# Turning the softmax weights of all eight heads of the second attention on VectorE, in a hybrid decoder trunk

## The chip, the core and the metric

The kernel runs on one core of a Trainium2 chip. The core has a matrix engine (TensorE, PE in the profile; PEld is its weight load), three engines for elementwise work (VectorE or DVE, ScalarE or ACT, GpSimd or POOL) and SyncE (SP), which here only issues transfers. Transfers are issued by SyncE and by ScalarE, each from its own list of instructions. Data lies in SBUF (128 partitions); TensorE writes into PSUM, of which this kernel uses eight banks. The metric is the time of one execution on the device, in microseconds.

## The reference

Two layers, each a mixer of three branches and an MLP, over 256 tokens of 1024 numbers:

```
h = rms_norm(x, attn_norm[l])
p = h @ w_in          # cq ckv k_rope | mq mk mv | rq rk rv rg | three gates
merged = sigmoid(g_mla)  * (mla(...)       @ w_branch_mla)
       + sigmoid(g_moba) * (moba(mq,mk,mv) @ w_branch_moba)
       + sigmoid(g_ret)  * (retention(rq,rk,rv,rg) @ w_branch_ret)
x = x + merged @ w_out
x = x + square(relu(rms_norm(x) @ w_mlp_up)) @ w_mlp_down
```

The second attention is `moba`: eight heads of 64. Its block is 256 tokens, as long as the sequence, so what is left of it is causal softmax attention of 256 queries on 256 keys. Retention has four heads with a decay in place of the softmax: scores times decay, times values, then a group norm per head, times silu of `rg`.

## The kernel before, in words

All activations are held turned: 128 rows of the model's dimension in the partitions, 256 tokens along the free axis. A product in full precision is made of three TensorE passes on rounded parts: each weight block comes from memory as `raw`, ScalarE rounds it to `whi` (line 210), VectorE makes the rest `wlo` (line 212), and TensorE adds three matmuls (lines 231 to 233), or, where the output is turned, a wide and a narrow one (lines 412 and 414). There are 7 `raw` buffers and 6 of `whi` and `wlo`. Line 195 is the load of a weight block, issued by SyncE.

The work of a layer is written as a list of units, `prog`, of one weight block each. Attention work is hung behind units with `at(slot, step)`. Around the change the units are, in order: the gates of the second attention (`gmoba1`, 4 blocks), the first attention's output (`bmla0`, `bmla1`, 2 each), retention's queries and keys (`rqk`, 4), its values (`rv`, 4), its gate (`rg`, 4), the second attention's output (`bmoba`, 4) and then retention's mixer gate (`gret`).

What the kernel lists is not the final order. Each engine has one list, fixed when the kernel is built: a planner simulates the engines' times and puts each instruction where its operands are ready by its own estimate, preferring what is written earlier. `keep_in_program_order` pins an instruction behind the one written before it on its engine; `manual_schedule` and, with it, `in_a_row` keep TensorE's part of some steps in the written order.

The second attention does its heads in two groups of four, `first` being the slot of `gmoba1`'s second block. Scores of heads 0 to 3 at `first`, of heads 4 to 7 eight units later (`GAP`). For each head VectorE adds the mask and takes the maximum (lines 498 and 501), ScalarE makes the exponential with its sum (line 507), VectorE divides (line 512): `prob`, 128 queries x 384 (one block for the first 128 queries, two for the others).

The product with the values needs the weights turned, keys in the partitions. There are two ways in the kernel before:

- heads 0 to 3 (`turned_blocks`, `moved_blocks`): VectorE turns 32x32 blocks within each quarter of the partitions (line 523) into one tile `blocks`; then sixteen transfers (line 563) of 32 partitions x 384 numbers, 48 KB each, exchange the blocks between quarters and give `probT`. Eight are issued by SyncE and eight by ScalarE, by turns, all pinned.
- heads 4 to 7 (`turned`): TensorE turns each 128x128 block against the identity, three per head (line 518), into a PSUM bank `ps_pt`, and ScalarE copies it to `probT` (line 519).

The first attention (`group is None`) turns all its heads the second way. `values` (lines 577 and 579) are the products with the values, into a bank `po`.

At the slot of `rg`'s second block one row of TensorE work is written: retention's scores (`ret_scores`, line 481, then line 998 on VectorE multiplies by the decay into `retA`), and then the two `values` steps of the second attention. `ret_values` (lines 1006 to 1008) use `retA` at the slot of `rg`'s last block. Retention's queries and keys pass through a rotation: four transfers each exchange quarters (line 434, `qkoth`), GpSimd and VectorE multiply by the tables and add (lines 446 and 449).

`blocks` lies in the buffer `KK`, of which there is one. It holds in turn the first attention's keys, `blocks`, then `gn` (retention's norm weights, loaded at line 1068 by a pinned SyncE transfer at `rv`'s first slot and used by GpSimd after `rg`), then half of the merged output.

Of the kernel before, what the change touches and what calls it, by code (L numbers as in the profile page):

```python
# [137 lines left out]
def trunk(ctx: ExitStack, tc: tile.TileContext, gx, wts, consts, gfin, gn, xtok, out):  # L138


    nc = tc.nc
# [76 lines left out]
    def acc_tile(name="acc"):  # L218
        return ps.tile([P, 512], F32, name=name, tag="acc", bufs=4)
# [31 lines left out]
    def split_plain(src, hi, lo):  # L251
        return nc.scalar.activation(hi, src, AF.Copy), nc.vector.tensor_sub(lo, src, hi.bitcast(F32))
# [98 lines left out]
    def project(l, key, xn, n, done=None, before=None, turns=(range(NT),)):  # L351

        accs, ws = [], []
        per = where[l, key, 0][1]
        count = KD // per

        def unit(i, ts, j):
            if not accs:
                accs.extend(acc_tile() for _ in range(NT))
            if before:  # L360
                before(i)
            if len(ws) <= j:
                ws.append(load_w(l, key, j))
            wh, wl = ws[j]
            for kk in range(per):
                k = per * j + kk
                ah, al = xn.k(k)
                for t in ts:
                    sl = slice(P * t, P * t + P)
                    three(accs[t][:, :n], ah[:, sl], al[:, sl], wh[:, kk, :], wl[:, kk, :], k == 0, k == KD - 1)  # L370
            if i == count * len(turns) - 1:
                done(accs)

        for turn, ts in enumerate(turns):
            for j in range(count):
                i = turn * count + j
                prog.append(((key, i), lambda i=i, ts=ts, j=j: unit(i, ts, j)))
# [87 lines left out]
    def in_a_row(*jobs):  # L465


        with tc.manual_schedule(engines={mybir.EngineType.PE}):
            rest = [job() for job in jobs]
        for job in rest:  # L470
            job()
# [14 lines left out]
    def attention_head(score, scale):  # L486


        got = {}

        def scores(s_ps=None):
            if s_ps is None:
                s_ps = misc_tile("ps_s")
                score(s_ps[:, 0:P], slice(0, P), slice(0, P))
                score(s_ps[:, P : 3 * P], slice(P, S), slice(0, S))
            p = sb.tile([P, 3 * P], F32, name="prob", bufs=4)
            m = small("smx")
            nc.vector.tensor_tensor_reduce(
                p[:, 0:P], s_ps[:, 0:P], mask[:, P : 2 * P], 1.0, NEG_INF, ALU.add, ALU.max, m[:, 0:1]
            )  # L500
            nc.vector.tensor_tensor_reduce(
                p[:, P : 3 * P], s_ps[:, P : 3 * P], mask, 1.0, NEG_INF, ALU.add, ALU.max, m[:, 1:2]
            )
            nc.vector.tensor_scalar(m[:, 2:4], m[:, 0:2], -scale, None, op0=ALU.mult)  # L504
            spans = ((0, P), (P, 3 * P))
            for i, (a, b) in enumerate(spans):
                nc.scalar.activation(  # L507
                    p[:, a:b], p[:, a:b], AF.Exp, bias=m[:, 2 + i : 3 + i], scale=scale, accum_out=m[:, 4 + i : 5 + i]
                )
            nc.vector.reciprocal(m[:, 6:8], m[:, 4:6])  # L510
            for i, (a, b) in enumerate(spans):
                nc.vector.tensor_scalar(p[:, a:b], p[:, a:b], m[:, 6 + i : 7 + i], None, op0=ALU.mult)
            got["p"] = p

        def turn(dst):
            pt = misc_tile("ps_pt")
            for i, src in enumerate((0, P, 2 * P)):
                nc.tensor.transpose(pt[:, P * i : P * i + P], got["p"][:, src : src + P], ident)  # L518
            nc.scalar.activation(dst, pt[:, : 3 * P], AF.Copy)

        def turn_blocks(dst):

            return nc.vector.transpose(dst, got["p"])

        return scores, turn, turn_blocks

    def attention(oT, score, vs, scale, first, group=None, former=None):

        tiles, pT = {}, {}

        def four_tile(h):
            if h // 4 not in tiles:
                tiles[h // 4] = sb.tile([P, 4 * 3 * P], F32, name="probT", bufs=2)
            return tiles[h // 4]

        def turned(h, turn):
            o = four_tile(h)[:, 3 * P * (h % 4) : 3 * P * (h % 4) + 3 * P]  # L540
            turn(o)
            pT[h] = o[:, 0:S], o[:, S : 3 * P]

        def turned_blocks(h, turn):

            if h == 0:
                pT["blocks"] = sb.tile([P, 4 * 3 * P], F32, name="blocks", tag="KK", bufs=1)
            by_head = (
                z.rearrange("p (c t h j) -> p h t c j", c=4, t=3, h=4)[:, h] for z in (pT["blocks"], four_tile(h))
            )  # L550

            tc.keep_in_program_order(turn(next(by_head)))
            o = next(by_head)
            pT[h] = o[:, 0:2], o[:, 2]

        def moved_blocks():

            e = 3 * P
            for a in range(4):
                for b in range(4):  # L560
                    src = pT["blocks"][32 * a : 32 * a + 32, e * b : e * b + e]
                    queue = (nc.sync, nc.scalar)[b % 2]
                    dma = queue.dma_start(four_tile(0)[32 * b : 32 * b + 32, e * a : e * a + e], src)
                    tc.keep_in_program_order(dma)

        def values(h0):


            o, v = acc_tile("po"), vs()
            for h in (h0 + 2, h0):  # L570
                cs = slice(S * (h - h0) // 2, S * (h - h0) // 2 + S)
                for i in range(2):
                    for j in (1, 0):
                        vh = v[i][:, VD * (h + j) : VD * (h + j) + VD]
                        dst = o[64 * j : 64 * j + 64, cs]
                        if i == 0:
                            nc.tensor.matmul(dst, vh, pT[h + j][0], start=True, stop=False)  # L577
                        else:
                            nc.tensor.matmul(dst[:, P:S], vh, pT[h + j][1], start=False, stop=True)
            dst = (part[:, h0 // 2 : h0 // 2 + 2, :].rearrange("p k s -> p (k s)") for part in oT)  # L580
            return lambda: split_plain(o, *dst)


        blocks = [lambda: values(4), lambda: values(0)]
        heads = [attention_head(lambda o, qs, ks, h=h: score(h, o, qs, ks), scale) for h in range(8)]
        if group is None:
            for h, (scores, turn, _) in enumerate(heads):
                at(first + h, scores)
                at(first + h + 2, lambda h=h, turn=turn: turned(h, turn))
            return blocks  # L590

        def four(h0):
            banks = group(h0)

            def rest():
                for h, bank in enumerate(banks, h0):
                    heads[h][0](bank)

            return rest


        at(first, lambda: in_a_row(*former, lambda: four(0)))
        at(first + GAP, lambda: in_a_row(lambda: four(4)))
        for h in range(4):
            at(first + TURN + h // 2, lambda h=h: turned_blocks(h, heads[h][2]))
            at(first + GAP + 3 + h // 2, lambda h=h + 4: turned(h, heads[h][1]))
        at(first + TURN + 1, moved_blocks)
        return blocks[::-1]

    def gates(l, key, xn):  # L610
# [52 lines left out]
    c = slice(G_END - 2 * KD, G_END + S)  # L663
# [35 lines left out]
    def at(slot, step):  # L699
        steps.setdefault(slot, []).append(step)  # L700

    def slot(key, j):
        return [k for k, _ in prog].index((key, j))
# [9 lines left out]
    def layer(l, xn, before):  # L713

        c0 = []
        c, mla, mqkv, rqkv = {}, {}, {}, {}
# [216 lines left out]
        first = slot("mv", 3)  # L933
# [23 lines left out]
        first = slot("gmoba1", 1)  # L957
        at(first, lambda: omobaT.extend((t4("omobah"), t4("omobal"))))

        def moba_scores(h0):  # L960
# [6 lines left out]
            return banks  # L967

        moba_last = attention(omobaT, None, lambda: mqkv["mv"], MB_D**-0.5, first, moba_scores, mla_last)


# [14 lines left out]
        rT, or_ps, aT, rg, oret = [], [], {}, {}, []  # L986
# [81 lines left out]
            tc.keep_in_program_order(nc.sync.dma_start(rg["gn"], src))  # L1068

        project(l, "rg", xn, 512, rg_done)  # L1070
        at(slot("rv", 0), load_gn)
        branch(l, "bmoba", omobaT, th_moba, merged)
        th_ret = gates(l, "gret", xn)
        order_out = ExitStack()
# [17 lines left out]
                merged_turn(0, i - 1)  # L1092

        branch(l, "bret", oretT, th_ret, merged, between)
        at(slot("rg", 1), lambda: in_a_row(ret_scores, *moba_last))
        for h in range(RT_H):
            at(slot("rg", 3), lambda h=h: ret_values(h))
        at(slot("rg", 3), group_norm)
# [218 lines left out]
    for l in range(L):  # L1317
        xn, before = layer(l, xn, before)
# [6 lines left out]
AHEAD = 1  # L1325
GAP = 8

TURN = 6
T4 = 8
RAW = 7  # L1330

# [79 lines left out]
```

## Time and profile before

| | us |
|---|---|
| median of 3 runs | 829.19 (828.47 to 829.30) |
| the profiled execution | 829.56 |
| its span, first to last instruction | 827.8 |
| TensorE busy | 821.3 |
| VectorE busy | 592.6 |
| ScalarE busy | 480.2 |
| GpSimd busy | 97.7 |

The granted TensorE clock is 0.999 of full speed over the span. The span is 1.8 us shorter than the execution, which has a start and an end around it. Rows of a timeline give the start, the time, the engine, the line, the operation, what it writes and reads, and how many instructions were merged into the row; a bracket gives the idle time ahead of it and what ended it. A q behind an engine's name means its list of issues, such as transfers.

### The profile page before, as it was taken

The page shows a single profiled execution, that of the slowest core. Times are in us where ns is not written, and L with a number is a line of the kernel's source. Part 1 is how long each engine was busy: PE and PEld are TensorE (multiplying, and loading weights), DVE is VectorE, ACT ScalarE, POOL GpSimd, SP SyncE. Part 2 cuts the span into 40 slices and gives each one's busy share as a digit, 9 for nine tenths or more (in the row PEclk, how much of TensorE's full clock was granted, in tenths as well). Part 3 has the DMA queues.
Part 4 walks back from the last instruction along what each step waited for, and adds up shares of the span by engine and source line. Part 5 has one row for each costly group of instructions (what it writes and reads, how often), then busy time and mean ns, then how long its engine had stood idle before and what let it go on. Part 6 is the DMA issues. An engine that isn't in the chain of part 4 may idle for free.

```text
span 827.8 us, 12148 instructions
## 1 busy us (share of the span) xinstructions
PE 821.3 (99%) x4339; PEld 699.1 (84%) x4339; DVE 592.6 (72%) x1067; ACT 480.2 (58%) x853; POOL 97.7 (12%) x75
## 2 busy tenths in 40 slices
PE   9999999999999999999999999999999999999997
PEld 7888878888888888888898888888888888888886
DVE  6877887795787566656697976877868766556663
ACT  7677664545556555555686575563555555555552
POOL 0100440230030000000035210023100300000000
PEclk9999999999999999999999999999999999999999
DMA  9966546736456666665557557565565666666611
GB/s 345 342 220 185 186 168 226 241 126 211 146 182 227 187 194 190 192 191 172 178 186 217 190 171 228 158 194 197 167 193 164 213 182 188 191 202 187 194 54 51
DMA packets 48060, 158.07 MB, mean 191 GB/s; under 512 B 6400, under 2 KB 8832, under 8 KB 47744
## 3 DMA queue, kind: packets, MB, share of 16 engines
q1 hardware_dynamic: 46656, 155.84, 59.3%
q10 hardware_dynamic: 1344, 1.46, 0.6%
q8 instruction: 34, 0.56, 0.3%
q14 instruction: 26, 0.21, 0.1%
HBM read 150.98 MB, written 1.05 MB: 184 GB/s over the span
## 4 chain that ended last, share of the span: by engine, by line
PE 99%; DVE 0%; ACT 0%; issue 0%; DVEq 0%
PE acc L231 18%; PE acc L233 18%; PE acc L232 18%; PE pup L1166 14%; PE pup L1168 7%; PE acc L1116 5%; PE acc L412 4%; PE acc L414 2%; PE ps_s L937 1%; PE acc L782 1%; PE ps_pt L518 1%; PE po L577 1%; PE ps_s L481 1%; PE warm L693 0%; PE acc L784 0%; PE pmt L1082 0%
## 5 line engine op out<-in xcount | busy, mean ns | idle before, releaser
L212 DVE TENSOR_TENSOR wlo<-raw,whi 128x1024 fp32r<-128x1024 f32 (+4 forms) x287 | 344.1, 1208 | 167.2 <-ACT whi L210 108.2
L210 ACT ACTIVATE whi<-raw 128x1024 fp32r<-128x1024 f32 (+4 forms) x287 | 290.9, 1023 | 177.4 <-PE acc L233 95.0
L1166 PE MATMUL pup<-xs,whi 128*128 128x512 f32 x504 | 123.5, 390 | 0.0
L233 PE MATMUL acc<-whi,xs 128*128 128x512 f32 (+1 forms) x304 | 119.5, 393 | 0.0
L232 PE MATMUL acc<-wlo,xs 128*128 128x512 f32 (+1 forms) x304 | 118.9, 391 | 0.0
L231 PE MATMUL acc<-whi,xs 128*128 128x512 f32 (+1 forms) x304 | 118.6, 394 | 0.0
L1166 PEld LDWEIGHTS pup<-xs,whi 128*128 128x128 f32 x504 | 93.4, 188 | 18.6
L231 PE MATMUL acc<-whi,sq 128*128 128x512 f32 x256 | 100.1, 391 | 0.0
L232 PE MATMUL acc<-wlo,sq 128*128 128x512 f32 x256 | 99.9, 390 | 0.0
L233 PE MATMUL acc<-whi,sq 128*128 128x512 f32 x256 | 98.5, 389 | 0.0
L1168 PE MATMUL pup<-xs,wlo 128*128 128x256 f32 x504 | 69.6, 283 | 0.0
L1168 PEld LDWEIGHTS pup<-xs,wlo 128*128 128x128 f32 x504 | 66.6, 191 | 3.1
L233 PEld LDWEIGHTS acc<-whi,xs 128*128 128x128 f32 x304 | 57.1, 188 | 11.5 <-issue 0.3
L231 PEld LDWEIGHTS acc<-whi,xs 128*128 128x128 f32 x304 | 57.1, 188 | 11.3 <-issue 0.7
L232 PEld LDWEIGHTS acc<-wlo,xs 128*128 128x128 f32 x304 | 57.1, 188 | 10.9
L233 PEld LDWEIGHTS acc<-whi,sq 128*128 128x128 f32 x256 | 48.0, 188 | 10.1
L1177 ACT ACTIVATE relu<-relu 128x256 f32<-128x256 f32 x64 | 25.5, 409 | 52.9 <-DVE relu L1176 52.9
L231 PEld LDWEIGHTS acc<-whi,sq 128*128 128x128 f32 x256 | 48.2, 188 | 9.2
L232 PEld LDWEIGHTS acc<-wlo,sq 128*128 128x128 f32 x256 | 48.2, 188 | 8.9
L288 POOL TENSOR_TENSOR sqsum<-sqsum,xsq 128x256 f32<-128x256 f32 x16 | 16.8, 1047 | 293.4 <-ACT xs L247 169.8
L507 ACT ACTIVATE prob<-prob,smx 128x128 f32<-128x128 f32 x64 | 28.4, 445 | 34.6 <-DVE smx L504 18.6
L446 POOL TENSOR_TENSOR qkoth<-qkoth,tab 128x512 f32<-128x512 f32 x12 | 23.3, 1944 | 161.1 <-DMA qkoth<-qkraw 161.1
(227 smaller groups left out, 1159.1 us busy)
## 6 DMA issues: line engine op xcount, KB each, us to landing
raw<-wts SPq DMA_DIRECT2D x264, 512.0 KB, 4.2
qkoth<-qkraw SPq DMA_DIRECT2D x48, 64.0 KB, 3.2
raw<-wts SPq DMA_DIRECT2D x5, 464.0 KB, 6.3
dec<-consts SPq DMA_DIRECT2D x2, 1024.0 KB, 7.4
raw<-wts SPq DMA_DIRECT2D x4, 416.0 KB, 3.2
raw<-wts SPq DMA_DIRECT2D x4, 256.0 KB, 4.3
xrow<-xtok SPq DMA_DIRECT2D x4, 256.0 KB, 7.1
gn<-gn SPq DMA_DIRECT2D x2, 512.0 KB, 4.1
```

Source lines behind the costliest of these rows:

```text
L210: nc.scalar.activation(hi[:, cs], raw[:, cs], AF.Copy)
L212: nc.vector.tensor_sub(lo[:, cs], raw[:, cs], hi[:, cs].bitcast(F32))
L231: nc.tensor.matmul(o, ah, bh, start=start, stop=False)
L232: nc.tensor.matmul(o, ah, bl, start=False, stop=False)
L233: nc.tensor.matmul(o, al, bh, start=False, stop=stop)
L412: nc.tensor.matmul(acc, wh[:, k, :], xn.both(k), start=k == 0, stop=False)
L446: mul = on.tensor_mul(*operands)
L507: nc.scalar.activation(p[:, a:b], p[:, a:b], AF.Exp, bias=m[:, 2 + i : 3 + i], scale=scale, accum_out=m[:, 4 + i : 5 + i])
L1116: nc.tensor.matmul(o, a, b, start=half == 0 and i == 0, stop=4 * half + n == KD and i == len(jobs) - 1)
L1166: nc.tensor.matmul(u, w, xm.both(k), start=k == 0, stop=False)
L1168: nc.tensor.matmul(u[:, 0:S], w, xm.k(k)[0], start=False, stop=k == KD - 1)
L1177: nc.scalar.activation(s, s, AF.Square)
```

## The change

Heads 4 to 7 of the second attention are turned like heads 0 to 3. `turned_blocks` now serves all eight, with a fresh tile `blocks` for each group; VectorE's instructions are pinned for the first group alone. `moved_blocks` is called once per group: the first group's sixteen transfers are all issued by SyncE, the second group's by SyncE and ScalarE by turns. The second group is turned at the slots where TensorE turned it before (11 and 12 units after `first`), and moved at the later of them, the slot of `rv`'s second block. `gn` follows in the same buffer, so its load is written at `rg`'s first slot instead of `rv`'s. In the row of TensorE work at `rg`'s second block, the second attention's values come first and retention's scores after them.

```diff
         def turned_blocks(h, turn):
 
-            if h == 0:
+            if h % 4 == 0:
                 pT["blocks"] = sb.tile([P, 4 * 3 * P], F32, name="blocks", tag="KK", bufs=1)
-            by_head = (
-                z.rearrange("p (c t h j) -> p h t c j", c=4, t=3, h=4)[:, h] for z in (pT["blocks"], four_tile(h))
+            turning, o = (
+                z.rearrange("p (c t h j) -> p h t c j", c=4, t=3, h=4)[:, h % 4] for z in (pT["blocks"], four_tile(h))
             )
-
-            tc.keep_in_program_order(turn(next(by_head)))
-            o = next(by_head)
+            turning = turn(turning)
+            if h < 4:
+
+                tc.keep_in_program_order(turning)
             pT[h] = o[:, 0:2], o[:, 2]
 
-        def moved_blocks():
+        def moved_blocks(h0):
...
-                    queue = (nc.sync, nc.scalar)[b % 2]
-                    dma = queue.dma_start(four_tile(0)[32 * b : 32 * b + 32, e * a : e * a + e], src)
+                    queue = nc.scalar if h0 and b % 2 else nc.sync
+                    dma = queue.dma_start(four_tile(h0)[32 * b : 32 * b + 32, e * a : e * a + e], src)
                     tc.keep_in_program_order(dma)
...
-        for h in range(4):
-            at(first + TURN + h // 2, lambda h=h: turned_blocks(h, heads[h][2]))
-            at(first + GAP + 3 + h // 2, lambda h=h + 4: turned(h, heads[h][1]))
-        at(first + TURN + 1, moved_blocks)
+        for i in range(2):
+            for h in range(4):
+                at(first + TURN[i] + h // 2, lambda h=4 * i + h: turned_blocks(h, heads[h][2]))
+            at(first + TURN[i] + 1, lambda i=i: moved_blocks(4 * i))
         return blocks[::-1]
...
-        at(slot("rv", 0), load_gn)
+        at(slot("rg", 0), load_gn)
...
-        at(slot("rg", 1), lambda: in_a_row(ret_scores, *moba_last))
+        at(slot("rg", 1), lambda: in_a_row(*moba_last, ret_scores))
...
-TURN = 6
+TURN = [6, GAP + 3]
```

## Prediction

> **What bounds the kernel now.** I read the page first: busy time by engine, then the chain that ended last, then which engine waits for whom.
>
> ```profile
> span 827.8 us, 12148 instructions
> ...
> PE 821.3 (99%) x4339; PEld 699.1 (84%) x4339; DVE 592.6 (72%) x1067; ACT 480.2 (58%) x853; POOL 97.7 (12%) x75
> ...
> PE 99%; DVE 0%; ACT 0%; issue 0%; DVEq 0%
> ```
>
> TensorE (PE) works for 821.3 of 827.8 us and is 99% of the chain that ended last. So a microsecond of TensorE work taken out is a microsecond of span, as long as nothing TensorE waits for becomes later than its place in TensorE's list. The rest of this text is about those two things: how much TensorE work goes, and whether the new, longer road of the softmax weights still arrives in time. All times below are from layer 0; layer 1 has the same pattern about 408 us later.
>
> The timeline of TensorE, where the transposes of heads 4 to 7 (line 518) stand among the matmuls of retention's value projection, and the same place in layer 1:
>
> ```profile
> 144.88 0.39 PE L231 MATMUL acc<-whi,xs 128*128 128x512 f32 x1
> 145.11 0.40 PE L232 MATMUL acc<-wlo,xs 128*128 128x512 f32 x1
> 145.34 0.49 PE L518 MATMUL ps_pt<-K,prob 128*128 128x128 f32 x3
> 145.59 0.48 PE L233 MATMUL acc<-whi,xs 128*128 128x512 f32 x1
> ...
> 147.28 0.48 PE L233 MATMUL acc<-whi,xs 128*128 128x512 f32 x1
> 147.59 0.40 PE L231 MATMUL acc<-whi,xs 128*128 128x512 f32 x1
> ...
> 552.74 0.40 PE L232 MATMUL acc<-wlo,xs 128*128 128x512 f32 x1
> ...
> 555.45 0.39 PE L232 MATMUL acc<-wlo,xs 128*128 128x512 f32 x1
> ```
>
> The reader is to see starts, not durations: each matmul lasts about 0.39 us, but the next starts 0.23 us after it (144.88 to 145.11).
>
> The timeline of SyncE's and ScalarE's queues and of VectorE over the same stretch, and the durations and landing times of the moves (line 563):
>
> ```profile
> 130.21 6.92 SPq L563 DMA_DIRECT2D probT<-blocks  x8
> 137.24 2.43 SPq L434 DMA_DIRECT2D qkoth<-qkraw  x4
> 140.34 0.46 SPq L195 DMA_DIRECT2D raw<-wts  x1
> 143.60 2.41 SPq L434 DMA_DIRECT2D qkoth<-qkraw  x4
> 146.12 21.29 SPq L195 DMA_DIRECT2D raw<-wts  x10
> ...
> 130.18 7.29 ACTq L563 DMA_DIRECT2D probT<-blocks  x8
> 137.51 0.40 ACT L507 ACTIVATE prob<-prob,smx 128x128 f32<-128x128 f32 x1 [8.24 <-DMA probT<-blocks]
> 141.56 4.86 ACT L210 ACTIVATE whi<-raw 128x1024 fp32r<-128x1024 f32 x5
> 146.31 1.73 ACT L519 ACTIVATE probT<-ps_pt 128x384 f32<-128x384 f32 x4
> ...
> 129.13 1.02 DVE L523 STREAM_TRANSPOSE blocks<-prob 128x384 f32<-128x384 f32 x2
> 134.34 0.37 DVE L504 TENSOR_SCALAR smx<-smx 128x2 f32<-128x2 f32 x4
> 138.53 0.17 DVE L510 RECIPROCAL smx<-smx 128x2 f32<-128x2 f32 x1 [3.83 <-ACT prob L507]
> 141.37 1.50 DVE L512 TENSOR_SCALAR prob<-prob,smx 128x128 f32<-128x128 f32 x2
> 144.65 5.75 DVE L212 TENSOR_TENSOR wlo<-raw,whi 128x1024 fp32r<-128x1024 f32 x5
> 151.59 0.69 DVE L449 TENSOR_TENSOR qkT<-qkT,qkoth 128x512 f32<-128x512 f32 x1 [1.19 <-POOL qkoth L446]
> ...
> SPq L563 <- DMA probT<-blocks: 2.0, 1, 2.0
> ...
> L563 SPq DMA_DIRECT2D probT<-blocks x8: 507/589/657, 130.2 to 136.5; - x8
> ...
> DMA to landing us min/median/max: 1.9/2.1/4.5
> ```
>
> The eight moves that ScalarE issues hold it for 7.3 us (130.18 to 137.47). Head 4's exponential stands behind them, and VectorE stands 3.83 us behind that. TensorE notices none of it.
>
> **The change part by part.**
>
> *Transposes off TensorE.* From 145.11 to 147.59 there are five steps between main matmuls; without the transposes they take 5 x 0.227 = 1.13 us, with them 2.48. So twelve transposes, with the changes to and fro, cost 1.35 us. In layer 1, 552.74 to 555.45 is six steps: 2.71 - 6 x 0.227 = 1.35 again. Both layers: **2.70 us off TensorE.** The reader may be tempted to price 24 transposes by their duration:
>
> ```profile
> L518 PE MATMUL ps_pt<-K,prob x72: 270/272/275, 73.9 to 555.1; 128*128 128x128 f32 x72
> ```
>
> That would be 24 x 0.272 = 6.5 us. I don't take it, since three of them in a row end 0.49 us after the first begins: they overlap. The Trainium skill's page "TensorE: Matmul & The Clock Gate" (Part 4: PE-mode transpose) gives about 275 ns for such a transpose inside a kernel, there for bf16; the trace agrees on the duration, and by it the saving would be an estimated 6.6 us, which the starts here contradict.
>
> *PSUM copies off ScalarE.* Four copies, 1.73 us a layer, go. ScalarE isn't on the chain, so this is worth nothing in the sum.
>
> *Four more block transposes on VectorE.* 4 x 0.51 = 2.0 us a layer by the row at 129.13. What hides it is the idle 3.83 us at 138.53: ScalarE no longer issues moves there, so its exponentials can begin when the maxima are ready (134.34 + 0.37 = 134.7) and not at 137.51, which brings everything after them forward by 2.8 us. If that cover were gone, the five `wlo` splits at 144.65 would start 2.0 us later. The first of them serves the first block of retention's gate. Its place on TensorE follows from the value projection, which begins here:
>
> ```profile
> 136.01 0.40 PE L231 MATMUL acc<-whi,xs 128*128 128x512 f32 x1
> 157.02 1.58 PE L481 MATMUL ps_r<-qkT 64*128 64x256 f32 x16
> 158.53 0.65 PE L577 MATMUL po<-probT,mv 128*64 128x256 f32 x4
> ...
> 161.28 0.50 PE L233 MATMUL acc<-whi,xs 128*128 128x512 f32 x1
> ...
> 163.70 0.38 PE L1006 MATMUL por<-rv,retA 128*128 128x128 f32 x2
> 166.30 0.48 PE L231 MATMUL acc<-whi,omobah 128*128 128x512 f32 x1
> ...
> 158.91 1.94 DVE L998 TENSOR_TENSOR retA<-ps_r,dec 128x384 f32<-128x384 f32 x4
> ```
>
> Four blocks of 12 matmuls are 48 x 0.227 = 10.9 us, so the gate's first block begins at 146.9 without the transposes. A fifth of 5.75 us after 144.65 its `wlo` is there, at 145.8: 1.1 us early, and 2.8 us more with the earlier exponentials. Taken as nothing; if both fail, 2.0 - 1.1 = 0.9 us a layer.
>
> *First group's moves all on SyncE.* The pace is 130.21 to 137.24 less the 2.0 us wait, over eight: 0.63 us each. Sixteen take 10.1 us, until 140.3, or 142.3 if the wait stays. Queued behind them are the four `qkoth` moves of retention's first pair, 3.1 to 5.1 us later than 137.24, and the weight load of 140.34. The second pair's `qkoth` moves wait for data until 143.6 anyway, and it is the second pair, rotated by GpSimd and VectorE at 151.59 + 0.69 = 152.3, that completes the scores' operands, which TensorE takes up at 157.02 (below): 4.7 us of cover for a late first pair. Weight loads: before, one load is issued between 130.2 and 146.1 and TensorE doesn't stop, so a hole of 16 us is covered by the seven `raw` buffers and the six split ones behind them. Nothing in the sum.
>
> *Second group's moves, new: eight on SyncE, eight on ScalarE.* They hold both queues about 7.3 us once more, and the loads of 146.12 begin up to that much later (a hole of some 23 us with few loads in it). The five `whi` made at 141.56 are 5 x 2.7 = 13.6 us of TensorE work (2.7 = 12 x 0.227), more than the 7.3. Bounds: nothing, or, if the cover were short, the rest of a hole; I take nothing, since thirteen blocks, 13 x 2.7 = 35 us of TensorE work, are in flight against 23.
>
> *`load_gn` four blocks later.* Its user is GpSimd, after the gate's projection at 163.5. Its buffer comes free when the second group has landed, 154 to 156 below; with the landing time of this transfer it is in place by 160:
>
> ```profile
> gn<-gn SPq DMA_DIRECT2D x2, 512.0 KB, 4.1
> ```
>
> Nothing in the sum.
>
> *The new road of heads 4 to 7, and values ahead of scores.* This is the part that can fail. Weights scaled at 141.37 + 1.50 = 142.9, less 2.8: 140.1. The one `blocks` buffer must be free of the first group: 140.3 to 142.3, plus 2.1 landing: 142.4 to 144.4. Four transposes: 144.4 to 146.4. Sixteen moves as measured, 7.3 + 2.1: **landed at 153.8 to 155.8.** The values stood at 158.53; 1.35 of transposes and 1.5 of scores (157.02 to 158.53) now lie behind or are gone, so at the same point of the gate's projection they begin at 155.7. And 161.28 to 163.70 shows 2.4 us of gate matmuls behind that can go ahead of them. So the data comes 0.1 us late to 1.9 early at the old point, and the list has 2.4 us of play. The order within the pair costs TensorE nothing in itself. Retention's weights (line 998) start 0.3 us after the scores end at 158.60 and the first is ready after another 0.5; the same 2.4 us of matmuls cover that 0.8. Sum: nothing, with bounds below.
>
> **Sum.** 2.70 us off, nothing added. The profiled execution took 829.56 us (span 827.8 and 1.8 around it), 0.37 above the median of the runs, 829.19. 829.56 - 2.70 = 826.86; on the median **826.5**.
>
> **Rivals.**
>
> *The moved weights come late.* The order of each engine is fixed when the kernel is built. If the values are placed right after the gate's second block, where the program writes them, that is 136.01 + 72 x 0.227 = 152.3, and TensorE stands there for the moves: 1.5 to 3.5 us a layer. It decides from 1.35 us a layer. With the middle, 2.5: 829.19 - 2.7 + 5.0 = **831.5**. For it: the move alone takes 9.4 us where a transpose and its copy took 2.3 (145.34 to 147.59). Against it: TensorE's list so far stands late against the data, not early: the transposes begin at 145.34 for weights complete at 142.87, and the program writes the scores after the gate's second block as well, which was 152.3 + 1.35 = 153.7, and they stand at 157.02, though their operands were complete at 152.3. The Trainium skill's page "VectorE: DVE Perf Modes" (Rules for kernel authors) says to turn 128x128 on TensorE where the result may land in PSUM, as it may here. By that rule the old way of heads 4 to 7 was the better one; the trace agrees that it is the shorter road, but not that the shorter road is what counts on a TensorE that never waits.
>
> *The cover is spent twice.* Late values use up the 2.4 us of gate matmuls, and then retention's values stand 0.8 us for their weights in each layer: 829.19 - 2.7 + 1.6 = **828.1**, which is no change.
>
> *Transposes worth their duration.* 829.19 - 6.5 = 822.7; the starts above speak against it.
>
> **How the numbers follow.** A measurement of this kernel can tell about 0.2%, 1.66 us, from no change. Forecast 826.5: 0.58. Cover spent twice, 828.1: 0.18. Late weights, 831.5: 0.22. Full duration: 0.02. Faster 0.60, same 0.18, slower 0.22. The likeliest case alone is 825.8 (0.7 below, as the lowest run stands to the median, 828.47 to 829.19) to 827.3. The range goes from there to the first part of the late case, 1.5 to 2 us a layer: 829.19 - 2.7 + 4 = 830.5.
>
> **What would show it.** Right: no row of line 519 for `mv`'s heads and 48 transposes instead of 72 on line 518; TensorE still 99%, its busy time 2.7 lower; the values (line 577) followed directly by the scores; ScalarE's first exponential of heads 4 to 7 about 2.8 us after the scores rather than 7; landing of the second group ahead of line 577's first start. Wrong: in the chain of waits a row of TensorE or its loader on `probT` moves, on `retA` or on `wlo`; a hole in TensorE's timeline around 153 to 164 and 560 to 572. The forecast falls if these holes reach 0.5 us a layer (no change) or 2.2 (slower).

## The result and the profile after

The changed kernel takes 826.02 us (median of 7 runs, 825.93 to 826.87) against 828.88 for the kernel before on the same chip (7 runs, 828.47 to 829.30): a ratio of 0.9968, 95% interval 0.9956 to 0.9979. Its profiled execution took 826.16 us, that of before 829.56.

The page of the changed kernel, with span, busy times and the chain that ended last, and in a fence of its own its view of TensorE's waits (what waited for what, us in total, times, longest):

```profile
span 824.4 us, 12153 instructions
...
PE 817.9 (99%) x4315; PEld 696.1 (84%) x4315; DVE 597.6 (72%) x1075; ACT 476.3 (58%) x845; POOL 97.7 (12%) x75
...
PE 99%; DVE 0%; ACT 0%; issue 0%; DVEq 0%
```

```profile
PE warm L695 <- PEq L1406: 0.8, 1, 0.8
```

TensorE is still 99% of the chain. It has 24 matmuls fewer, and the only wait left is the one of 0.8 us in its warm-up. VectorE is 5.0 us busier, ScalarE 3.9 less.

The span is 3.4 us shorter, but not all of that is the change. To see where it went I cut the span at matmuls that both kernels have: the first one on `omlah` (the first attention's output) and the first one on `oreth` (retention's output). Between them lie all the edits. TensorE's timeline, the kernel before first, then the changed one:

```profile
112.27 0.39 PE L231 MATMUL acc<-whi,omlah 128*128 128x512 f32 x1
...
199.93 0.39 PE L231 MATMUL acc<-whi,oreth 128*128 128x512 f32 x1
...
520.58 0.39 PE L231 MATMUL acc<-whi,omlah 128*128 128x512 f32 x1
...
608.23 0.39 PE L231 MATMUL acc<-whi,oreth 128*128 128x512 f32 x1
```

```profile
111.48 0.39 PE L231 MATMUL acc<-whi,omlah 128*128 128x512 f32 x1
...
197.84 0.39 PE L231 MATMUL acc<-whi,oreth 128*128 128x512 f32 x1
...
518.50 0.39 PE L231 MATMUL acc<-whi,omlah 128*128 128x512 f32 x1
...
604.83 0.39 PE L231 MATMUL acc<-whi,oreth 128*128 128x512 f32 x1
```

The stage goes from 87.66 to 86.36 us in layer 0 (197.84 - 111.48) and from 87.65 to 86.33 in layer 1: 1.30 and 1.32 us off, 2.62 together. The other 0.8 us lies ahead of 112.27, where nothing was edited. The first scores of the first attention start at 64.33 us in the kernel before and at 63.55 in the changed one, and in the kernels below this start lies anywhere between 63.26 and 64.38, whatever was edited. So one profiled execution differs from another by up to 1.1 us there, and the stages tell more than the spans. Every time of layer 0 in the changed kernel is to be read 0.8 us later when it is set beside one of before.

The timeline of SyncE's and ScalarE's issues and of VectorE in the changed kernel, layer 0:

```profile
129.44 11.23 SPq L565 DMA_DIRECT2D probT<-blocks  x16
140.78 4.96 SPq L434 DMA_DIRECT2D qkoth<-qkraw  x8
145.84 5.02 SPq L565 DMA_DIRECT2D probT<-blocks  x8
150.96 1.00 SPq L195 DMA_DIRECT2D raw<-wts  x2
152.29 0.33 SPq L1070 DMA_DIRECT2D gn<-gn  x1
...
133.74 0.40 ACT L507 ACTIVATE prob<-prob,smx 128x128 f32<-128x128 f32 x1 [0.98 <-DVE smx L504]
...
144.75 5.16 ACTq L565 DMA_DIRECT2D probT<-blocks  x8
150.01 1.27 ACT L979 ACTIVATE rv<-acc,ms 128x512 f32<-128x512 f32 x2 [5.34 <-DMA probT<-blocks]
...
137.59 0.55 DVE L512 TENSOR_SCALAR prob<-prob,smx 128x128 f32<-128x128 f32 x2
...
142.16 1.50 DVE L523 STREAM_TRANSPOSE blocks<-prob 128x384 f32<-128x384 f32 x3 [0.53 <-issue]
```

The reader is to see the new road in order: the first sixteen moves hold SyncE until 140.7; the exponentials of heads 4 to 7 no longer wait behind moves on ScalarE (133.74, before 137.51), and their weights are scaled by 138.1; VectorE turns them at 142.16, when the first group should have landed and left `blocks` free (its last move is issued at 140.1, and a move lands 1.9 to 2.0 us after its issue); the second sixteen moves go out between 144.75 and 150.9. The landing times and GpSimd's wait for `gn`, from the view of transfers in this stretch and from GpSimd's timeline:

```profile
probT<-blocks SPq DMA_DIRECT2D x24, 48.0 KB, 1.9
...
gn<-gn SPq DMA_DIRECT2D x1, 512.0 KB, 6.5
```

```profile
158.87 1.69 POOL L1063 TENSOR_TENSOR rgb<-rg,gn 128x512 f32<-128x512 f32 x1 [10.02 <-DMA gn<-gn]
```

The last move is issued at 150.3 or so and lands 1.9 us later, at 152.2. TensorE in the changed kernel, layer 0:

```profile
156.79 0.39 PE L233 MATMUL acc<-whi,xs 128*128 128x512 f32 x1
157.11 0.65 PE L579 MATMUL po<-probT,mv 128*64 128x256 f32 x4
...
158.46 0.60 PE L579 MATMUL po<-probT,mv 128*64 128x256 f32 x4
...
159.86 1.58 PE L481 MATMUL ps_r<-qkT 64*128 64x256 f32 x16
161.37 0.50 PE L231 MATMUL acc<-whi,omobah 128*128 128x512 f32 x1
161.70 0.39 PE L232 MATMUL acc<-wlo,omobah 128*128 128x512 f32 x1
...
166.51 0.38 PE L1008 MATMUL por<-rv,retA 128*128 128x128 f32 x2
```

The values start at 157.11, behind the whole of retention's gate projection. Those of heads 0 to 3 come first; those of heads 4 to 7, which need the second group, start at 158.46, 6.3 us after it landed. The scores follow directly, and behind them the second attention's output projection (`omobah`), not the rest of the gate; retention's values come at 166.51.

### The profile page after: what moved, and what is told of

Read it like the earlier page. It is cut to its first block, busy times and chain, and to the rows that moved or that the text cites. A ratio compares the mean times of both kernels' runs of the same rounds, so it can differ in the third digit from the quotient of the medians.

```text
span 824.4 us, 12153 instructions
## 1 busy us (share of the span) xinstructions
PE 817.9 (99%) x4315; PEld 696.1 (84%) x4315; DVE 597.6 (72%) x1075; ACT 476.3 (58%) x845; POOL 97.7 (12%) x75
## 4 chain that ended last, share of the span: by engine, by line
PE 99%; DVE 0%; ACT 0%; issue 0%; DVEq 0%
PE acc L231 18%; PE acc L233 18%; PE acc L232 18%; PE pup L1168 14%; PE pup L1170 7%; PE acc L1118 5%; PE acc L412 5%; PE acc L414 2%; PE ps_s L939 1%; PE acc L784 1%; PE po L579 1%; PE ps_s L481 1%; PE ps_pt L518 1%; PE warm L695 0%; PE acc L786 0%; PE po L581 0%
## 5 line engine op out<-in xcount | busy, mean ns | idle before, releaser
L212 DVE TENSOR_TENSOR wlo<-raw,whi 128x1024 fp32r<-128x1024 f32 (+4 forms) x287 | 347.6, 1219 | 165.4 <-ACT whi L210 105.9
L412 PE MATMUL acc<-xs,whi 128*128 128x512 f32 x160 | 40.5, 395 | 0.0
```

The source lines that it names most:

```text
L212: nc.vector.tensor_sub(lo[:, cs], raw[:, cs], hi[:, cs].bitcast(F32))
L412: nc.tensor.matmul(acc, wh[:, k, :], xn.both(k), start=k == 0, stop=False)
```

## The experiments

The stage from the first `omlah` matmul to the first `oreth` matmul, worked out from TensorE's starts as above, for all kernels (the column ahead of it is the first attention, from its first scores to the first `omlah` matmul). All other stages agree within 0.05 us, but for the start; rounding can move a stage by 0.01. The kernels ran on several chips, each beside the kernel before, whose median there lay between 828.73 and 829.00, and each ratio is to the kernel before on the same chip. The stages come from one profiled execution of each kernel.

| kernel | median, us (runs) | ratio to before, 95% interval | layer 0: first attention, stage | layer 1: first attention, stage |
|---|---|---|---|---|
| before | 828.88 (7) | | 47.94, 87.66 | 56.21, 87.65 |
| changed | 826.02 (7) | 0.9968, 0.9956 to 0.9979 | 47.94, 86.36 | 56.20, 86.33 |
| order undone | 826.70 (7) | 0.9971, 0.9960 to 0.9982 | 47.94, 86.49 | 56.25, 86.64 |
| order alone | 829.07 (11) | 1.0000, 0.9991 to 1.0009 | 47.94, 87.65 | 56.24, 87.65 |
| turned twice | 831.26 (8) | 1.0028, 1.0018 to 1.0038 | 47.94, 88.93 | 56.25, 88.91 |
| all moves by turns | 827.25 (11) | 0.9979, 0.9970 to 0.9988 | 47.94, 86.68 | 56.24, 86.68 |
| values pinned behind the gate's 2nd block | 825.87 (5) | 0.9964, 0.9951 to 0.9976 | 47.94, 86.29 | 56.25, 86.29 |
| values pinned behind the gate's 1st block | 828.52 (11) | 0.9995, 0.9986 to 1.0004 | 47.94, 87.39 | 56.25, 86.71 |
| half of the first attention too | 831.58 (6) | 1.0032, 1.0020 to 1.0044 | 50.86, 90.83 | 54.82, 86.33 |
| all of the first attention too | 830.99 (11) | 1.0020, 1.0009 to 1.0030 | 46.59, 90.08 | 59.05, 86.39 |
| that half in layer 1 alone | 825.08 (5) | 0.9952, 0.9940 to 0.9965 | 47.94, 86.36 | 54.75, 86.33 |
| the same, with values pinned behind the 2nd block | 824.99 (5) | 0.9953, 0.9939 to 0.9966 | 47.94, 86.29 | 54.82, 86.33 |

**The order, undone and alone.** The changed kernel with the scores first again:

```diff
-        at(slot("rg", 1), lambda: in_a_row(*moba_last, ret_scores))
+        at(slot("rg", 1), lambda: in_a_row(ret_scores, *moba_last))
```

> The changed kernel with retention's scores ahead of the second attention's values again; all else as changed. Theory (only the 24 transposes count, everything else is covered): 826.0 us, within 0.8 of the changed kernel; 48 transposes on TensorE, no idle time of TensorE. Rival (the order is what makes the new road fit): the values stand later by the 1.5 us of scores, the second attention's output matmuls start later, and TensorE stands for them, 1 us or more a layer: 828 us or more.

and the kernel before with the values first:

```diff
-        at(slot("rg", 1), lambda: in_a_row(ret_scores, *moba_last))
+        at(slot("rg", 1), lambda: in_a_row(*moba_last, ret_scores))
```

> The kernel before with nothing changed but the order: values ahead of retention's scores; heads 4 to 7 still turned on TensorE. Theory: 828.9, no change within 0.8, since the order adds and removes no TensorE work and nothing waits. Rival (part of the gain is the order's): 827.5 or less.

Alone the order is worth nothing: 1.0000, and 87.65 in both stages. Undone, the stages are 0.13 and 0.31 us longer. The larger loss is seen on TensorE in layer 1 of that kernel:

```profile
563.69 0.39 PE L581 MATMUL po<-probT,mv 128*64 128x128 f32 x4
564.01 0.50 PE L232 MATMUL acc<-wlo,xs 128*128 128x512 f32 x1
564.34 0.40 PE L233 MATMUL acc<-whi,xs 128*128 128x512 f32 x1
564.67 0.65 PE L579 MATMUL po<-probT,mv 128*64 128x256 f32 x4
```

The values stand in two pieces with two main matmuls between. Changing between main and attention matmuls has a price: the three steps here are 0.32, 0.33 and 0.33 us. In the changed kernel a step from a line 581 row to the next value row takes 0.22 and a step between main matmuls 0.23, so each is 0.10 longer, which together is the 0.31. (The changed kernel pays the same at the two ends of its one row: 0.32 from 156.79 to 157.11, and 0.33 from 161.37 to 161.70.) What the order brings here, then, is a tidier list and no wait avoided; the two ratios, 0.9968 and 0.9971, have intervals that overlap.

**What a transpose costs.** The kernel before, with the transposes of heads 4 to 7 of the second attention made twice, so 12 more in each layer:

```diff
-    def attention_head(score, scale):
+    def attention_head(score, scale, times=1):
...
-            for i, src in enumerate((0, P, 2 * P)):
+            for i, src in [(i, src) for _ in range(times) for i, src in enumerate((0, P, 2 * P))]:
...
-        heads = [attention_head(lambda o, qs, ks, h=h: score(h, o, qs, ks), scale) for h in range(8)]
+        heads = [attention_head(lambda o, qs, ks, h=h: score(h, o, qs, ks), scale, 2 if group else 1) for h in range(8)]
```

> The kernel before with each transpose of heads 4 to 7 made twice on TensorE, 24 more over two layers. It measures the price of a transpose by itself. Theory (price is the step from start to start, 1.35 us for twelve): 828.9 + 2.7 = 831.6. Rival (price is the duration of 0.272 us): 828.9 + 6.5 = 835.4. Rival (the transposes were partly hidden and the gain came from elsewhere): 829 to 830.

It took 831.26 us, 2.3 more than the kernel before on its chip (829.0). The stages grew by 1.27 and 1.26. Its timeline, where all 24 of layer 0 stand in one row:

```profile
144.43 2.78 PE L518 MATMUL ps_pt<-K,prob 128*128 128x128 f32 x24
146.97 0.47 PE L233 MATMUL acc<-whi,xs 128*128 128x512 f32 x1
```

From 144.43 to 146.97 are 2.54 us for 24, so 0.106 us each, though each is 272 ns long in the profile. Twelve cost 1.27 by that, and the changes to and fro come on top. The price by duration is out: 12 more would have cost 3.3 us a layer. The Trainium skill's page "TensorE: Matmul & The Clock Gate" (Part 4: PE-mode transpose) gives about 275 ns for one, by which the 24 would be an estimated 6.6 us; the duration here agrees with it, the cost on a full TensorE does not, and the measurement decides.

**All moves by turns.** The changed kernel with the first group's moves on both queues as before:

```diff
-                    queue = nc.scalar if h0 and b % 2 else nc.sync
+                    queue = (nc.sync, nc.scalar)[b % 2]
```

> The changed kernel with the first group's moves issued by SyncE and ScalarE by turns, as before the change. ScalarE's exponentials of heads 4 to 7 stand behind eight moves again, about 3 us later, and with them the second group. Theory (the second group lands about 4 us ahead of the values, so 3 us later still fits): 826.0, within 0.8. Rival (the queue is what makes it fit): the second group lands after its place, 1 to 3 us a layer on TensorE: 828 to 832.

827.25 us; the stages are 0.32 and 0.35 us longer than in the changed kernel. TensorE and SyncE in layer 0:

```profile
150.24 0.65 PE L579 MATMUL po<-probT,mv 128*64 128x256 f32 x4
...
159.62 0.65 PE L579 MATMUL po<-probT,mv 128*64 128x256 f32 x4
...
147.19 6.38 SPq L565 DMA_DIRECT2D probT<-blocks  x8
```

The second group's moves end at 153.6, where the changed kernel has 150.9; this kernel's first attention began 0.8 us later (64.38), so the moves themselves are 1.9 us later. And the planner put the values of heads 0 to 3 at 150.24 and those of heads 4 to 7 at 159.62. No wait appears on TensorE. So the queue matters through the order that the planner makes of it: one more interruption of the main matmuls by values costs about 0.3 us a layer, as above.

**Values as early as they are written.** The prediction's main rival was that the values would stand right behind the gate's second block. Here the gate's third block is pinned behind the row of values and scores:

```diff
-    def three(o, ah, al, bh, bl, start, stop):
-        nc.tensor.matmul(o, ah, bh, start=start, stop=False)
+    def three(o, ah, al, bh, bl, start, stop, pin=lambda mm: mm):
+        pin(nc.tensor.matmul(o, ah, bh, start=start, stop=False))
...
-                    three(accs[t][:, :n], ah[:, sl], al[:, sl], wh[:, kk, :], wl[:, kk, :], k == 0, k == KD - 1)
+                    three(accs[t][:, :n], ah[:, sl], al[:, sl], wh[:, kk, :], wl[:, kk, :], k == 0, k == KD - 1, *[tc.keep_in_program_order][: key == "rg" and i == 2 and kk == 0])
```

> The changed kernel with the values and retention's scores held at the place where they are written, right behind the gate's second block (the gate's third block is pinned behind them), instead of where the planner put them, behind the gate's last block. In the changed kernel's trace of layer 0 this place is at about 151.5, the copies of retention's values that free the banks end at 151.3, and the last move lands at 152.2, while the values of heads 4 to 7 come 1.3 us after those of heads 0 to 3. Theory (the moves land some 4 us ahead of the planner's place): nothing waits even here: 826.0, within 0.8. Rival of the prediction (late weights, priced there at 1.5 to 3.5 us a layer): 829 to 833.

and in the next kernel its second block, so that the values stand 12 matmuls earlier still:

```diff
-                    three(accs[t][:, :n], ah[:, sl], al[:, sl], wh[:, kk, :], wl[:, kk, :], k == 0, k == KD - 1, *[tc.keep_in_program_order][: key == "rg" and i == 2 and kk == 0])
+                    three(accs[t][:, :n], ah[:, sl], al[:, sl], wh[:, kk, :], wl[:, kk, :], k == 0, k == KD - 1, *[tc.keep_in_program_order][: key == "rg" and i == 1 and kk == 0])
...
-        at(slot("rg", 1), lambda: in_a_row(*moba_last, ret_scores))
+        at(slot("rg", 0), lambda: in_a_row(*moba_last, ret_scores))
```

> The same row of TensorE work held one block of the gate earlier still, at about 148.8 in layer 0. Theory: now TensorE must stand, in layer 0 about 1.8 to 2.1 us for the bank that ScalarE's copies of retention's values free at 150.6 and for the moves at 152.2, in layer 1 0 to 0.3 us, since its place is 555.8 against copies ended at 555.1 and moves landed at 557.4: 826.0 + 2.2 = 828.2, range 827 to 829.5. If nothing changes here either, the cover is larger than read; if it costs 4 us or more, the wait of the prediction's rival is dearer than it was priced.

Behind the second block there is no wait: 825.87 us, stages of 86.29 in both layers. TensorE there:

```profile
151.06 0.39 PE L233 MATMUL acc<-whi,xs 128*128 128x512 f32 x1
151.38 0.65 PE L579 MATMUL po<-probT,mv 128*64 128x256 f32 x4
...
154.13 1.58 PE L481 MATMUL ps_r<-qkT 64*128 64x256 f32 x16
```

The step of 0.32 into the values is that of the changed kernel, and so is the length from there to the scores (2.75 us). The second group's last move is issued at 149.3 in that kernel and lands at 151.2, and the values of heads 4 to 7 begin at 152.7, 1.5 us later. One block earlier there are waits. In that kernel the timelines of TensorE and ScalarE, and then the other row of TensorE's waits:

```profile
150.04 0.65 PE L579 MATMUL po<-probT,mv 128*64 128x256 f32 x4 [0.62 <-ACT rv L979]
...
149.30 1.26 ACT L979 ACTIVATE rv<-acc,ms 128x512 f32<-128x512 f32 x2 [4.21 <-DMA probT<-blocks]
```

```profile
PE po L579 <- ACT whi L210: 0.4, 2, 0.2
```

The longest wait isn't for the moves. It is for a PSUM bank: `po` needs one that ScalarE frees by copying retention's values out (line 979), and these copies stand 4.2 us behind the second group's moves on ScalarE. The two waits of 0.2 us are those of heads 4 to 7; the profile puts them down to a rounding on ScalarE, which the values don't use. In layer 0 the last move is issued at 149.5 and so lands at 151.5, and the wait ends at 151.76; that the moves are what it waits for is likely, but not shown. The stages are 1.03 and 0.38 us longer than in the changed kernel. The medians say 2.5 (828.52 against 826.02). Of the other 1.1, 0.4 is a later start in the profiled execution (63.95 against 63.55); that execution took 828.04, below the median of runs that spread from 827.91 to 829.60, and what made the others longer isn't known. What is settled: the changed kernel has room down to the written place, which is 24 gate matmuls or 5.4 us ahead of the one that the planner chose, and the edge lies within the block before it.

**More heads the same way.** If 12 transposes are worth 1.3 us, the first attention has 24 of them in each layer. Heads 4 to 7 of it, on top of the change:

```diff
         if group is None:
-            for h, (scores, turn, _) in enumerate(heads):
+            for h, (scores, turn, turn_b) in enumerate(heads):
                 at(first + h, scores)
-                at(first + h + 2, lambda h=h, turn=turn: turned(h, turn))
-            return blocks
+                at(first + h + 2 + 2 * (h // 4) - (h % 4 + 1) // 2 * (h // 4), (lambda h=h, turn=turn: turned(h, turn)) if h < 4 else (lambda h=h, turn=turn_b: turned_blocks(h, turn)))
+            at(first + 9, lambda: moved_blocks(4)); return blocks
```

> The changed kernel, and heads 4 to 7 of the first attention turned the same way: 24 transposes fewer on TensorE over both layers, 32 moves more (eight on SyncE and eight on ScalarE a layer), 8 block transposes more on VectorE. Theory (a transpose taken off TensorE is worth its step of 0.11 us as long as the weights land in time; here they have five blocks, 13.6 us, from their turning to the values): 826.0 - 2.6 = 823.4, within 0.8. Rival (VectorE is too full here: the page shows it eight to nine tenths busy in this stretch): TensorE comes to wait for split weights, 826 or more.

831.58 us. Layer 1 gains what another 12 transposes are worth (56.20 to 54.82). Layer 0 loses 2.9 us in the first attention and 4.5 behind it. The waits of TensorE in that kernel, and the timelines of SyncE, ScalarE and TensorE:

```profile
PE acc L231 <- ACT omlah L252: 4.0, 1, 4.0
PE po L579 <- ACT th L619: 1.8, 1, 1.8
```

```profile
95.32 6.82 SPq L565 DMA_DIRECT2D probT<-blocks  x8
102.18 10.75 SPq L434 DMA_DIRECT2D qkoth<-qkraw  x16
...
102.57 4.11 ACT L210 ACTIVATE whi<-raw 128x1024 fp32r<-128x1024 f32 x4 [6.77 <-DMA probT<-blocks]
...
111.87 0.69 ACT L619 ACTIVATE th<-acc,half 128x512 f32<-128x512 f32 x1 [4.04 <-POOL qkT L449]
...
114.76 0.63 PE L232 MATMUL acc<-wlo,omlah 128*128 128x512 f32 x1
115.18 0.63 PE L231 MATMUL acc<-whi,omlah 128*128 128x512 f32 x1
```

Here the cover was gone. ScalarE's weights stood 6.8 us behind the moves, sixteen `qkoth` transfers queued behind SyncE's moves, GpSimd's rotation waited for these, ScalarE for GpSimd, and TensorE stood 1.8 and 4.0 us. Behind the 4.0 TensorE then ran slowly: steps of 0.43 us instead of 0.23. The view of that kernel by stretches (length, then busy time and instruction count of PE, PEld, DVE, ACT and POOL, the granted clock, the share of DMA, GB/s):

```profile
112.00:120.00 8.00, 5.83 (x14) 4.58 (x15) 1.38 (x2) 2.11 (x4) 8.00 (x7) 0.57 0.83 290
120.00:128.00 8.00, 8.00 (x46) 6.23 (x45) 6.42 (x19) 2.64 (x5) 5.17 (x4) 1.00 0.46 144
```

The clock is 0.57 over 112 to 120 and full again behind it. The slow steps last from 114.2 to 119.9; at 0.43 instead of 0.227 that loses 5.7 x (1 - 0.227 / 0.43) = 2.7 us. With the two waits, 1.8 + 4.0, and less the 1.4 that the twelve transposes are worth (layer 1 shows it), this makes 7.1 of the 7.4 us that layer 0 lost. That the order of the queues alone makes the chain is read from the trace, not tried by itself.

All eight heads of the first attention, with a buffer of its own for their first group, and one `raw` weight buffer and one small work buffer (`W2K`) fewer to make room for it:

```diff
-    pT["blocks"] = sb.tile([P, 4 * 3 * P], F32, name="blocks", tag="KK", bufs=1)
+    pT["blocks"] = sb.tile([P, 4 * 3 * P], F32, name="blocks", tag="KK" if h or group else "own", bufs=1)
...
-            for h, (scores, turn, _) in enumerate(heads):
+            for h, (scores, _, turn) in enumerate(heads):
                 at(first + h, scores)
-                at(first + h + 2, lambda h=h, turn=turn: turned(h, turn))
-            return blocks
+                at(first + (4, 4, 5, 5, 8, 8, 9, 9)[h], lambda h=h, turn=turn: turned_blocks(h, turn))
+            at(first + 5, lambda: moved_blocks(0)); at(first + 9, lambda: moved_blocks(4)); return blocks
...
-W2K = 17
+W2K = 16
...
-RAW = 7
+RAW = 6
```

> All sixteen heads of both attentions turned on VectorE; no softmax transpose on TensorE at all. The first group of the first attention needs a buffer of its own, paid for with one raw buffer (7 to 6) and one small work buffer (17 to 16). Theory: another 2.6 us: 820.8, if six raw buffers still cover SyncE's longer holes. Rival: moves and fewer buffers starve the weight loads, TensorE waits for split weights: 824 or more.

830.99 us: fewer transposes than in any kernel here, and slower than before. TensorE waits 2.9 us ahead of the first `omlah` matmul of layer 0 and 3.9 us ahead of the first attention's values in layer 1 (until 514.69), and the granted clock is 0.994 over the span, as in the kernel above, where the changed one has 0.998. Behind the 2.9 the clock is at half, as TensorE's timeline and the view by stretches show:

```profile
109.85 0.79 PE L231 MATMUL acc<-whi,omlah 128*128 128x512 f32 x1 [2.90 <-ACT omlah L252]
```

```profile
110.00:112.00 2.00, 2.00 (x5) 1.61 (x6) 1.24 (x3) 1.90 (x3) 2.00 (x2) 0.50 0.46 108
```

Since this edit takes buffers away too, it doesn't say which part costs what.

The half that paid, alone: heads 4 to 7 of the first attention in layer 1 only,

```diff
...
+                at(first + h, scores); on_dve = l == 1 and h >= 4
+                at(first + (8 + (h - 4) // 2 if on_dve else h + 2), (lambda h=h, turn=turn_b: turned_blocks(h, turn)) if on_dve else (lambda h=h, turn=turn: turned(h, turn)))
+            at(first + 9, (lambda: moved_blocks(4)) if l == 1 else (lambda: None)); return blocks
...
```

> The changed kernel, with heads 4 to 7 of the first attention turned on VectorE in layer 1 alone. In e7 the stretch of the first attention in layer 1 became shorter by 1.38 us (56.20 to 54.82) while layer 0 lost 7 us. Theory (the price of a transpose holds wherever the moves find free queues, and the loss of e7 was layer 0's, where sixteen rope transfers stand behind the moves on SyncE): 826.0 - 1.4 = 824.6, within 0.8. Rival (the loss is general, and layer 1 was spared by chance of the list): 826 or more.

and the same with the pin of the gate's third block from above added:

```diff
+                    three(accs[t][:, :n], ah[:, sl], al[:, sl], wh[:, kk, :], wl[:, kk, :], k == 0, k == KD - 1, *[tc.keep_in_program_order][: key == "rg" and i == 2 and kk == 0])
```

> e9 and e5 in one kernel: layer 1's half of the first attention turned on VectorE, and the second attention's values held at the place where they are written. Theory: the two don't touch each other, 825.9 - 1.4 = 824.5, within 0.8; it would be the fastest version here, or equal to e9. Rival (the two want the same cover): 825.5 or more.

825.08 and 824.99 us. TensorE's only wait in either is the one of 0.8 us in its warm-up, as in the changed kernel; in the first of the two the values of layer 1's first attention begin at 510.04 with no gap ahead of them.

Layer 1's first attention takes 54.75 instead of 56.20 us, 1.45 less, and every other stage is that of the changed kernel. The loss in layer 0 is gone with the edit there. Against the kernel before it is 0.9952 (0.9940 to 0.9965). The interval overlaps that of the change itself, so that it beats the changed kernel is shown by the stage of one profile and supported by the lower median, not by the ratios. The pin adds nothing that can be told (0.07 us in layer 0's stage).

## Why the prediction was right, and where its steps were not

Said: 826.5, in a range of 825.8 to 830.5. Measured: 826.02, against 828.88 for the kernel before by seven runs, where the prediction had started from 829.19 by three.

**Transposes off TensorE.** Said: 2.70 us, by starts and not by durations. Measured: 1.30 + 1.32 = 2.62 in the stages, 2.86 by the medians, and 2.53 for the reverse edit, 12 transposes more in each layer. The rival of the full duration is shown wrong. What makes the last 0.08 us isn't known; the list of TensorE was also put together anew around the values.

**PSUM copies.** Worth nothing, as said: ScalarE is 3.9 us less busy and nobody gains by it.

**Block transposes on VectorE.** The cover was what the prediction named. ScalarE's first exponential came 3.0 us earlier (137.51 less the 0.8 of the start is 136.7; it began at 133.74), and no `wlo` is waited for. The bound of 0.9 us a layer wasn't touched.

**First group on SyncE.** Said: 10.1 us, until 140.3, or 142.3 with a wait, to be read as 139.5 to 141.5 here. Measured: 11.2 us, until 140.7. A wait of 2.0 us as before doesn't appear as such; one of the issues took 1.8 us instead. The `qkoth` transfers began 4.3 us later than before (said: 3.1 to 5.1), and the scores began long after their operands were whole.

**Second group and weight loads.** Said: 7.3 us on both queues. Measured: 5.0 on SyncE and 5.2 on ScalarE, because neither row has a wait inside: each is eight issues of about 0.6 us, where the 7.3 of before held some 2 us more than its eight issues take. This is the term that was mis-sized, and it fell on the good side: landing at 152.2, or 153.0 on the scale of before, where the prediction had 153.8 to 155.8. The hole in the weight loads was about 22.8 us (128.1 to 151.0), as said, and TensorE didn't notice it. One thing was not on the list: ScalarE's copies of retention's values stand behind its moves, 5.3 us (150.01), and they hold PSUM banks. At the chosen place this costs nothing; with the values behind the gate's first block it is the first wait to appear.

**`load_gn`.** Said: in place by 160. It was issued at 152.29 and took 6.5 us, so 158.8. GpSimd did wait for it, 0.9 us beyond `rg` (ready at 157.9), in a place where TensorE doesn't depend on it soon enough to notice.

**Place of the values.** Said: 155.7 on the scale of before, with data between 0.1 us late and 1.9 early and 2.4 us of play. Measured: 157.9 on that scale, behind all of the gate, and the data 4.9 us early. The prediction carried the old place forward by subtraction; the planner had set it anew. It also set the landing against the first start of the values, where heads 4 to 7 come 1.35 us behind (158.46). And the work behind which retention's weights hide was not the rest of the gate, which by then was done, but the second attention's output projection: 5.1 us of it (161.37 to 166.51) for an `retA` that began 1.4 us after the scores. In the kernel before, retention's values went ahead of that projection. So the conclusion held, with the wrong name for its cover: that nothing waited at the place where the planner put the values was foreseen by a reckoning that didn't describe that place, and in that part it was luck. That the moves would have been in time at the written place too is what the pinned kernel adds.

**The rivals.** Late weights were priced for the written place at 1.5 to 3.5 us a layer. With the values pinned there the wait is nil. So the rival failed twice: the planner didn't put them there, and there they would have been in time, because the moves land up to 2.8 us earlier than was reckoned and heads 4 to 7 are needed 1.35 us later. The case begins within the block before, and its first and longest wait is for a bank, not for a move. The cover spent twice didn't occur. The rule of the Trainium skill's page "VectorE: DVE Perf Modes" (Rules for kernel authors), to turn 128x128 on TensorE where the result may go to PSUM, is right here about the length of the road and not about the time; in the kernel with half of the first attention moved too, layer 0 shows the place where its side wins.

## What to carry to other kernels

On a kernel whose TensorE never stops, price work taken off it by the step between starts, not by the duration of a row (0.106 against 0.272 us here). Look at the steps around an interruption too: a second piece of the values cost about 0.3 us here, while the four groups of transposes in layer 0 of the kernel before cost 1.35 in all, where twelve at 0.106 make 1.27. The longer road that takes its place is free only while all that queues behind its transfers has cover: look at what stands behind the moves on each issuing engine, the PSUM copies and the other branch's transfers too, for each place by itself, since the same edit gained 1.4 us in one layer and lost 7.4 in the other. Where a planner orders the engines, don't carry an old place forward by subtraction; give both ends, and find the edge by pinning.

## What was not expected of the hardware

When TensorE had stood for 4.0 us, in the kernel with half of the first attention moved too, its granted clock was about half for the next 5.7 us (0.57 over the stretch of 112 to 120, where it stood for the first 2.2, and steps of 0.43 instead of 0.227 us), which made a wait of 4.0 us cost 6.7. In the kernel with all of the first attention moved, a wait of 2.9 us had the clock at 0.50 from its end at 109.85 to about 113.1, and behind one of 3.9 us the clock fell to 0.50 only at about 516, 1.2 us after TensorE had gone on at 514.69, and stayed there until about 519. Shorter waits had no such trail: after the 1.8 us ahead of the values in the first of these kernels (until 107.31) the clock is 1.00 from 108 to 112, and behind the 0.6 us in the kernel with the values behind the gate's first block it is 1.00 from 150 to 158. The Trainium skill's page "TensorE: Matmul & The Clock Gate" (Why this matters for your kernels) says to leave no gap of more than about 3 us between bursts of matmuls, or the clock falls to half. The traces agree: 2.9 us and more do it, 1.8 doesn't, and no run here shows where between them the edge is.
